# Moving the conditioning's multiplications from VectorE to ScalarE

## The chip, the cores and the metric

The kernel runs on one core of a Trainium2 chip. The metric is the device time of one execution in microseconds (us), lower is better. Work is issued in program order to five engines that run side by side: TensorE (PE; matmuls and, as PEld, weight loads), VectorE (DVE), ScalarE (ACT), GpSimd (POOL) and SyncE (SP). Each engine works through its own queue in order and waits on semaphores for the others. Transfers from HBM are issued from SP, ACT or POOL; a transfer stands in that engine's queue until its buffer is free, and then runs by itself.

## What the kernel computes

A two-layer encoder trunk on 256 tokens of width 1024. Each layer has a token mixer (three gated branches) and a PEER channel mixer (128x128 experts, top 16 of each of 8 heads). Both are conditioned by a vector c through adaLN:

```
cond = silu(c)
ada = cond @ w_ada[l] + b_ada[l]            # 1024 -> 6 x 1024, a matrix-vector product
sh1, sc1, g1, sh2, sc2, g2 = split(ada, 6)
u = x * (1 + sc1) + sh1;  x = LN(ALPHA * x + g1 * mixer(u))
u = x * (1 + sc2) + sh2;  x = LN(ALPHA * x + g2 * peer(u))
```

`w_ada` has 2 x 1024 x 6144 numbers, 50 MB. The change touches the product `cond @ w_ada` alone, and of it the part that is done beside other work.

## The kernel before

All large products are matmuls on TensorE in a split fp32 form. A weight tile of 128x1024 arrives by an SP transfer (`raw`, three buffers). ScalarE copies it to the rounded `hi` (L86), and VectorE or GpSimd subtracts to get `lo` (L88), as an item of the plan says ("v" or "g"). `Stream.get` (L98 to L110) does this two items ahead of TensorE: `hi` and `lo` have three buffers each, so the split of item i+2 starts when TensorE has finished item i-1, and the next `raw` load into a buffer waits until that item's split is done.

The stages in order: the mixer of layer 0 (projections, attention, long convolution, branches, output), up to about 400 us; PEER of layer 0, with the `u` stream (128 items against expert_u, to about 880 us) and the `v` stream (128 items against expert_v, L1550, to about 1240 us); then both again for layer 1. In the `v` loop each pair of items first prepares the two expert weights of the next pair: `hi` of P on ScalarE (L1494), `lo` of P on VectorE (L1495). Then each item is split ahead, multiplied (12 matmuls), and followed by one step of the conditioning, `self.ada(last, 1)` at L1523. In the same loop of layer 0, from about 1100 us on, the filters and loads of layer 1 run as background generators, pumped a step at a time (`self.bg.pump`).

The conditioning is cut into blocks (layer l, part j, half h) of eight tiles of 128x512, k = 0 to 7. The first two parts of layer 0 are done in `start` by other code. The other 20 blocks, 160 tiles, are done a tile at a time by `ada`, called once after each weight item in the mixer of layer 0 (L1095, L1120, L1140, L1165, L1216: 6 blocks), in the `v` loop of layer 0 (12 blocks) and at the beginning of that of layer 1 (2 blocks). The tiles have three buffers (`adaw`). A call at tile p first calls `ada_load` (L385), which issues, from the ACT queue, the transfers of all tiles up to p+2 that haven't been issued: in steady state one, that of tile p+2, into the buffer of tile p-1, for which it waits until VectorE has used tile p-1. Then VectorE multiplies tile p by column k of cond and adds it to the block's sum `acc` (one buffer): a TENSOR_SCALAR for k = 0 (L416), a SCALAR_TENSOR_TENSOR for the others (L418). After k = 7 one call does nothing and the next calls `ada_column` (L423): four PE transposes of `acc`, and two small VectorE operations. So a block takes ten calls.

Of the kernel before, what the change touches and what calls it, by code (L numbers as in the profile page):

```python
# [9 lines left out]
F32 = mybir.dt.float32  # L10
# [4 lines left out]
AF = mybir.ActivationFunctionType  # L15
ALU = mybir.AluOpType
# [140 lines left out]
class Trunk:  # L157
# [72 lines left out]
    def setup(self):  # L230
        nc, a = self.nc, self.a
        c = self.const
        self.ada_todo = [(l, j, k, h) for l in range(DEPTH) for j in range(6) for h in range(2) for k in range(8)
                         if (l, j) > (0, 1)]
        self.ada_tiles = {}
        self.ada_pos = self.ada_next = 0
        self.ada_done = None
        cc = c.tile([128, 8], F32, name="cc")
        self.load(cc, a["c"])
        self.ident = c.tile([128, 128], F32, name="ident")  # L240
        self.load(self.ident, a["ident"])
        self.bcol = c.tile([128, DEPTH, 6, 8], F32, name="bcol")
        self.load(self.bcol, a["bada"])
        self.new_x()
        self.open_layer(0)
        self.cond = c.tile([128, 8], F32, name="cond")
        e = c.tile([128, 8], F32, name="ce")
        nc.scalar.activation(out=e, in_=cc, func=AF.Exp, scale=-1.0)
        nc.vector.tensor_scalar(out=e, in0=e, scalar1=1.0, scalar2=None, op0=ALU.add)
        nc.vector.reciprocal(out=e, in_=e)  # L250
        nc.vector.tensor_tensor(out=self.cond, in0=cc, in1=e, op=ALU.mult)
        dp = self.ctx.enter_context(self.tc.tile_pool(name="dp", bufs=1, space=bass.MemoryType.DRAM))
        self.spill = dp.tile([128, 2, 1024], F32, name="spill")
        self.uh = self.keep.tile([128, 8, 256], F32R, name="uh")
        self.ul = self.keep.tile([128, 8, 256], F32R, name="ul")
        self.adac = c.tile([128, DEPTH, 6, 8], F32, name="adac")
        self.gbc = None
        for j in (1, 4):
            nc.vector.tensor_scalar(out=self.bcol[:, :, j, :], in0=self.bcol[:, :, j, :], scalar1=1.0, scalar2=None,
                                    op0=ALU.add)  # L260
# [134 lines left out]
    def ada(self, until, most=1000):  # L395

        nc = self.nc
        while most:
            if self.ada_done:
                self.ada_wait -= 1  # L400
                if self.ada_wait == 0 or most > 100:
                    self.ada_column()
                most -= 1
                continue
            if self.ada_pos == len(self.ada_todo) or self.ada_todo[self.ada_pos][:2] > until:
                return
            l, j, k, h = self.ada_todo[self.ada_pos]
            self.ada_load()
            w = self.ada_tiles.pop(self.ada_pos)
            self.ada_pos += 1  # L410
            most -= 1
            if k == 0:
                self.acc = self.sm.tile([128, 512], F32, tag="acc", name="acc", bufs=1)
            acc = self.acc
            if k == 0:
                nc.vector.tensor_scalar(out=acc, in0=w, scalar1=self.cond[:, 0:1], scalar2=None, op0=ALU.mult)  # L416
            else:
                nc.vector.scalar_tensor_tensor(out=acc, in0=w, scalar=self.cond[:, k:k + 1], in1=acc,  # L418
                                               op0=ALU.mult, op1=ALU.add)
            if k == 7:  # L420
                self.ada_done, self.ada_wait = (l, j, h), 2

    def ada_column(self):  # L423

        nc = self.nc
        l, j, h = self.ada_done
        self.ada_done = None
        s = slice(h * 4, h * 4 + 4)
        t = self.adac[:, l, j, s]
        p = self.bp((128, 4, 128))  # L430
        for m in range(4):
            nc.tensor.transpose(p[:, m, :], self.acc[:, m * 128:m * 128 + 128], self.ident)
        nc.vector.tensor_reduce(out=t, in_=p, op=ALU.add, axis=AX.X)
        nc.vector.tensor_tensor(out=t, in0=t, in1=self.bcol[:, l, j, s], op=ALU.add)
# [1269 lines left out]
```

## Time and profile before

| | |
|---|---|
| time, median of 3 runs | 2453.06 us (2447.99 to 2457.54) |
| the profiled execution's own time | 2454.66 us |
| its span, first to last instruction | 2452.6 us |
| mean granted clock of TensorE | 0.974 |
| PE busy | 2290.2 us, 93% |
| DVE busy | 1857.4 us, 76% |
| ACT busy | 1169.3 us, 48% |
| POOL busy | 874.7 us, 36% |
| DMA, mean | 179 GB/s |

Busy time is the time in which an engine executes an instruction, whether or not anything waits for it. The chain of waits says what the end hangs on: followed back from the last instruction, at each step to what released it. Its share of "issue" is time for which the profile shows no reason. The averages mix stages with different limits, so the views by stretch count more than this table.

### The profile page before, as it was taken

To read this page: it belongs to the slowest core of one execution; us is meant where nothing else is said; L and a number is where in the kernel's file an instruction comes from. 1 tells how busy PE (TensorE), PEld (TensorE's weight loads), DVE (VectorE), ACT (ScalarE), POOL (GpSimd) and SP (SyncE) were. 2 spreads that over 40 slices of the span, in tenths; PEclk is the share of its full clock that TensorE was granted. 3 is DMA by queue.
4 is the path that set the end of the run, shared out by engine and by line. 5 is a ranking of instruction groups with operands and counts; after the bars stand their busy time and mean duration, and the time that the engine had idled before them with its cause. 6 is when DMAs were issued, how large, how long until landed. Compare 5 with 4: busy or idle time off the path is not lost.

```text
span 2452.6 us, 38276 instructions
## 1 busy us (share of the span) xinstructions
PE 2290.2 (93%) x14400; PEld 2014.9 (82%) x14400; DVE 1857.4 (76%) x3196; ACT 1169.3 (48%) x1860; POOL 874.7 (36%) x403
## 2 busy tenths in 40 slices
PE   6899978979999999998899999899899999999997
PEld 4688657979999988885667886689899999888886
DVE  6886796977788878876975656879677887766676
ACT  4444434545555444443445444455455554444443
POOL 3521535660000024445754327557300000444563
PEclk9999998989999999998999999999999999999999
DMA  7553554545555578886664434444455555766664
GB/s 284 172 157 108 175 177 146 164 129 164 165 164 166 170 232 267 264 262 224 199 223 127 133 100 154 170 132 147 146 166 168 163 167 172 243 195 190 213 199 153
DMA packets 132592, 438.44 MB, mean 179 GB/s; under 512 B 16369, under 2 KB 17741, under 8 KB 130360
## 3 DMA queue, kind: packets, MB, share of 16 engines
q1 hardware_dynamic: 103328, 377.01, 48.6%
q10 hardware_dynamic: 26968, 51.23, 6.5%
q0 software_dynamic: 2112, 7.77, 0.9%
q8 instruction: 113, 1.85, 0.3%
q14 instruction: 71, 0.58, 0.1%
HBM read 432.80 MB, written 3.15 MB: 178 GB/s over the span
## 4 chain that ended last, share of the span: by engine, by line
PE 69%; DVE 21%; issue 3%; DMA 2%; ACT 2%; POOL 1%; ACTq 0%; SPq 0%; DVEq 0%; POOLq 0%
PE bg L209 26%; PE pj L1550 25%; PE pj L197 8%; DVE lo L88 2%; PE pj L209 2%; DVE acc L418 1%; DVE eq L1322 1%; PE gp L1449 1%; PE gp L1450 1%; PE bg L662 1%; ACT hi L86 1%; DVE eq L1317 1%; POOL lo L88 1%; DVE x L1254 1%; PE pj L1018 1%
## 5 line engine op out<-in xcount | busy, mean ns | idle before, releaser
L88 POOL TENSOR_TENSOR lo<-raw,hi 128x1024 fp32r<-128x1024 f32 x272 | 693.4, 2554 | 1489.0 <-ACT hi L86 1449.7
L86 ACT ACTIVATE hi<-raw 128x1024 fp32r<-128x1024 f32 x688 | 726.2, 1058 | 459.3 <-PE pj L1550 227.3
L209 PE MATMUL bg<-uh,hi 128*128 128x256 f32 x2240 | 645.0, 288 | 5.9 <-ACT hi L86 5.9
L1550 PE MATMUL pj<-hi,P 128*128 128x512 f32 x2048 | 641.6, 395 | 6.2 <-DVE P L1495 3.5
L88 DVE TENSOR_TENSOR lo<-raw,hi 128x1024 fp32r<-128x1024 f32 x416 | 543.9, 1308 | 134.2 <-ACT hi L86 127.9
L209 PE MATMUL bg<-uh,lo 128*128 128x256 f32 x2240 | 637.6, 285 | 8.2 <-POOL lo L88 8.2
L209 PE MATMUL bg<-ul,hi 128*128 128x256 f32 x2240 | 636.8, 284 | 0.0
L1550 PEld LDWEIGHTS pj<-hi,P 128*128 128x128 f32 x2048 | 387.2, 190 | 92.6 <-DVE P L1495 4.8
L209 PEld LDWEIGHTS bg<-uh,lo 128*128 128x128 f32 x2240 | 433.1, 193 | 9.4 <-POOL lo L88 9.4
L209 PEld LDWEIGHTS bg<-uh,hi 128*128 128x128 f32 x2240 | 433.4, 193 | 6.4 <-ACT hi L86 6.3
L209 PEld LDWEIGHTS bg<-ul,hi 128*128 128x128 f32 x2240 | 433.4, 193 | 0.1
L1550 PE MATMUL pj<-lo,P 128*128 128x512 f32 x1024 | 404.2, 395 | 12.2 <-DVE lo L88 8.0
L1495 DVE TENSOR_TENSOR P<-b,P 128x512 fp32r<-128x512 f32 x128 | 257.7, 2014 | 117.7 <-ACT P L1494 117.5
L1550 PEld LDWEIGHTS pj<-lo,P 128*128 128x128 f32 x1024 | 194.4, 190 | 58.9 <-DVE lo L88 11.6
L197 PE MATMUL pj<-hi,uh 128*128 128x512 f32 x432 | 190.6, 441 | 7.2 <-DVE mt L1175 3.1
L1479 ACT ACTIVATE bg<-bg 128x256 f32<-128x256 f32 (+24 forms) x208 | 56.8, 273 | 290.8 <-PE bg L209 290.8
L197 PE MATMUL pj<-lo,uh 128*128 128x512 f32 x432 | 176.0, 407 | 14.2 <-DVE lo L88 8.8
L197 PE MATMUL pj<-hi,ul 128*128 128x512 f32 x432 | 176.2, 408 | 9.0 <-DVE ul L1235 7.7
L418 DVE SCALAR_TENSOR_TENSOR acc<-adaw,cond,acc 128x512 f32<-128x512 f32 x140 | 141.1, 1008 | 4.1 <-DMA adaw<-in_wada 2.2
L1456 DVE SCALAR_TENSOR_TENSOR b<-gp,b 128x160 f32<-128x160 f32 (+6 forms) x236 | 58.8, 310 | 103.3 <-ACT b L1454 103.3
L197 PEld LDWEIGHTS pj<-lo,uh 128*128 128x128 f32 x432 | 85.4, 198 | 35.0 <-DVE lo L88 10.3
L197 PEld LDWEIGHTS pj<-hi,uh 128*128 128x128 f32 x432 | 85.1, 197 | 33.5 <-issue 7.4
(317 smaller groups left out, 2854.4 us busy)
## 6 DMA issues: line engine op xcount, KB each, us to landing
raw<-in_u SPq DMA_DIRECT2D x256, 512.0 KB, 3.5
raw<-in_v SPq DMA_DIRECT2D x256, 512.0 KB, 4.2
raw<-in_wtok SPq DMA_DIRECT2D x92, 512.0 KB, 3.6
adaw<-in_wada ACTq DMA_DIRECT2D x160, 256.0 KB, 3.7
raw<-in_whyd SPq DMA_DIRECT2D x24, 512.0 KB, 3.6
raw<-in_wq SPq DMA_DIRECT2D x24, 512.0 KB, 3.8
raw<-in_wbr SPq DMA_DIRECT2D x20, 512.0 KB, 3.7
su<-in_wada SPq DMA_DIRECT2D x8, 1024.0 KB, 10.5
```

What stands on the lines that cost most here:

```text
L86: self.nc.scalar.activation(out=h, in_=t, func=AF.Copy)
L88: eng.tensor_tensor(out=w, in0=t, in1=h.bitcast(F32), op=ALU.subtract)
L197: self.nc.tensor.matmul(psums[T], l[:, k, s], m[:, kk, :], start=(k == 0 and j == 0), stop=(k == K - 1 and j == 2))
L209: self.nc.tensor.matmul(ps, m[:, k, :], x[:, k, :], start=(k == 0 and j == 0), stop=(k == 7 and j == 2))
L418: nc.vector.scalar_tensor_tensor(out=acc, in0=w, scalar=self.cond[:, k:k + 1], in1=acc, op0=ALU.mult, op1=ALU.add)
L662: nc.tensor.matmul(ps[P], self.fwd[:, P, c, :], z[:, P, :], start=True, stop=True)
L1018: self.nc.tensor.matmul(ps[T], x[:, 2 * i + kk, ts], w[:, kk, :], start=x is self.uh and i + kk + part == 0, stop=x is self.ul and i + kk ...
L1254: nc.vector.max_index(out=i[:, 8:16], in_max=v[:, 8:16], in_values=s)
L1456: nc.vector.scalar_tensor_tensor(out=t[:, :, ts], in0=pr[:, i:j, :], scalar=1.0 / GATE_UNIT, in1=t[:, :, ts], op0=ALU.mult, op1=ALU.mult)
L1479: nc.scalar.activation(out=p[:, 0:n], in_=p[:, 0:n], func=AF.Gelu)
L1495: nc.vector.tensor_tensor(out=w, in0=src, in1=h.bitcast(F32), op=ALU.subtract)
L1550: self.nc.tensor.matmul(self.vacc[T][h], x[:, s], v[:, w], start=start and c == 0, stop=stop and c == 2)
```

## The change

`ada` no longer multiplies on VectorE. A new function `ada_product(i)` issues an ACTIVATE (Copy with the column of cond as a per-partition scale) on ScalarE: for k = 0 it writes the product straight into `acc`, for the others in place over the tile. A call at tile p makes sure that tile p has its product, and, unless p is the block's last, that of tile p+1 too. VectorE then adds tile p to `acc` with a TENSOR_TENSOR (nothing for k = 0). `ada_load` is now called from `ada_product`, only when a product is issued; what it loads is unchanged (all tiles up to two past the current one).

```diff
-        self.ada_pos = self.ada_next = 0
+        self.ada_pos = self.ada_next = self.ada_scaled = 0
 ...
             l, j, k, h = self.ada_todo[self.ada_pos]
-            self.ada_load()
+            self.ada_product(self.ada_pos)
+            if k < 7:
+                self.ada_product(self.ada_pos + 1)
             w = self.ada_tiles.pop(self.ada_pos)
             self.ada_pos += 1
             most -= 1
-            if k == 0:
-                self.acc = self.sm.tile([128, 512], F32, tag="acc", name="acc", bufs=1)
-            acc = self.acc
-            if k == 0:
-                nc.vector.tensor_scalar(out=acc, in0=w, scalar1=self.cond[:, 0:1], scalar2=None, op0=ALU.mult)
-            else:
-                nc.vector.scalar_tensor_tensor(out=acc, in0=w, scalar=self.cond[:, k:k + 1], in1=acc,
-                                               op0=ALU.mult, op1=ALU.add)
+            if k:
+                nc.vector.tensor_tensor(out=self.acc, in0=w, in1=self.acc, op=ALU.add)
             if k == 7:
                 self.ada_done, self.ada_wait = (l, j, h), 2
+
+    def ada_product(self, i):
+
+        if i < self.ada_scaled:
+            return
+        self.ada_scaled = i + 1
+        self.ada_load()
+        w, k = self.ada_tiles[i], self.ada_todo[i][2]
+        out = w
+        if k == 0:
+            out = self.acc = self.sm.tile([128, 512], F32, tag="acc", name="acc", bufs=1)
+        self.nc.scalar.activation(out=out, in_=w, func=AF.Copy, scale=self.cond[:, k:k + 1])
```

## Rows read from the trace of the kernel before

**Rows 1.** Busy time in three stretches: stretch, length, each engine, PEclk, DMA share, GB/s.
```profile
60.00:400.00 340.00, 297.95 (x1504) 237.80 (x1504) 266.86 (x436) 144.11 (x241) 135.67 (x60) 0.94 0.49 156
...
870.00:1100.00 230.00, 228.79 (x1056) 190.53 (x1055) 185.27 (x166) 110.78 (x129) 95.19 (x39) 1.00 0.81 261
1100.00:1260.00 160.00, 140.58 (x552) 103.89 (x551) 125.31 (x130) 71.79 (x90) 93.49 (x58) 0.94 0.68 219
```
**Rows 2.** The same stretches, VectorE's busy time on the conditioning's tiles alone.
```profile
60.00:400.00 340.00, 55.16 (x48) 0.94 0.49 156
...
870.00:1100.00 230.00, 45.66 (x64) 1.00 0.81 261
1100.00:1260.00 160.00, 40.58 (x32) 0.94 0.68 219
```
**Rows 3.** Chain of waits by line, 60 to 400 us, then 1100 to 1260 us.
```profile
by line: PE pj L197 27.8%; issue 10.7%; DVE acc L418 6.8%; DVE lo L88 5.9%; PE pj L209 5.2%; PE bg L662 4.0%; DMA raw<-in_wout 2.6%; DVE r L686 1.9%; DVE sq L629 1.8%; PE bg L604 1.8%; PE bg L753 1.5%; PE bg L809 1.5%; ACT hi L86 1.4%; PE b
...
by line: PE pj L1550 43.7%; issue 10.4%; DVE acc L418 7.1%; DMA w<-in_hy_w 5.5%; DVE lo L88 5.0%; PE bg L662 4.3%; DVE P L1495 3.2%; DMA adaw<-in_wada 3.2%; PE bg L604 3.0%; DVE sq L629 2.4%; DVE hh L578 2.1%; DVE acc L416 1.6%; POOL lo L88
```
**Rows 4.** Single lines on VectorE: ns min/median/max of one, first and last start.
```profile
L418 DVE SCALAR_TENSOR_TENSOR acc<-adaw,cond,acc x140: 735/751/2984, 76.1 to 2133.1; 128x512 f32<-128x512 f32 x140
L416 DVE TENSOR_SCALAR acc<-adaw,cond x20: 475/480/2614, 74.1 to 2116.3; 128x512 f32<-128x512 f32 x20
...
L1495 DVE TENSOR_TENSOR P<-b,P x128: 675/2467/4090, 879.5 to 2425.6; 128x512 fp32r<-128x512 f32 x128
```
**Rows 5.** Groups of instructions on ScalarE: count, busy us, mean ns, idle before.
```profile
L607 ACT ACTIVATE hh<-ld,nt 128x512 f32<-128x512 f32 x16 | 11.0, 720 | 6.7 <-DVE acc L418 6.7
...
L619 ACT ACTIVATE sq<-hh 128x512 f32<-128x512 f32 x16 | 9.5, 620 | 10.6 <-DVE acc L418 10.2 <-DVE sq L629 0.4
```
**Rows 6.** Transfers of adaw, issue to landing: 60 to 400, 870 to 1100, 1100 to 1260 us.
```profile
DMA to landing us min/median/max: 2.5/3.3/7.3
...
DMA to landing us min/median/max: 2.6/4.0/5.6
...
DMA to landing us min/median/max: 2.5/3.7/9.2
```
**Rows 7.** Timeline in the v stream: start, length, instruction, idle before; two items of a pair.
```profile
979.53 1.06 ACT L86 ACTIVATE hi<-raw 128x1024 fp32r<-128x1024 f32 x1 [1.14 <-PE pj L1550]
979.61 0.33 ACTq L392 DMA_DIRECT2D adaw<-in_wada  x1
...
980.83 1.21 DVE L88 TENSOR_TENSOR lo<-raw,hi 128x1024 fp32r<-128x1024 f32 x1
...
982.25 1.06 ACT L86 ACTIVATE hi<-raw 128x1024 fp32r<-128x1024 f32 x1 [1.66 <-PE pj L1550]
...
983.22 0.62 ACT L1494 ACTIVATE P<-b 128x512 fp32r<-128x512 f32 x1
...
983.39 2.41 POOL L88 TENSOR_TENSOR lo<-raw,hi 128x1024 fp32r<-128x1024 f32 x1 [3.03 <-ACT hi L86]
...
983.87 2.48 DVE L1495 TENSOR_TENSOR P<-b,P 128x512 fp32r<-128x512 f32 x1 [0.38 <-ACT P L1494]
```
**Rows 8.** Timeline where a block of the conditioning ends and the next begins.
```profile
955.08 0.34 ACTq L392 DMA_DIRECT2D adaw<-in_wada  x1
...
962.75 1.06 ACT L86 ACTIVATE hi<-raw 128x1024 fp32r<-128x1024 f32 x1 [1.14 <-PE pj L1550]
962.83 0.33 ACTq L392 DMA_DIRECT2D adaw<-in_wada  x1
...
965.88 1.06 ACT L86 ACTIVATE hi<-raw 128x1024 fp32r<-128x1024 f32 x1 [2.07 <-PE pj L1550]
...
967.02 2.42 POOL L88 TENSOR_TENSOR lo<-raw,hi 128x1024 fp32r<-128x1024 f32 x1 [3.45 <-ACT hi L86]
```
**Rows 9.** Who waited for whom, 870 to 1100, then 1100 to 1260: us, times, longest.
```profile
ACT hi L86 <- DMA raw<-in_v: 24.1, 14, 2.3
...
ACT P L1494 <- DVE acc L416: 7.3, 1, 7.3
```

## The prediction

> **What bounds the kernel now.** I read the busy time by stretch first, then the chain of waits of the stretches in which the conditioning runs, then its single instructions, then the timeline of the v stream. The 160 tiles fall into four places: 48 in the mixer of layer 0 (60 to 400 us), 64 in the saturated v stream (870 to 1100), 32 in its second half (1100 to 1260), 16 at the start of layer 1's v stream. The reader should see that these differ. From 870 to 1100 TensorE is busy 228.79 of 230 us at a granted clock of 1.00 [rows 1]: nothing taken from VectorE can shorten it. From 60 to 400 and 1100 to 1260 TensorE has gaps (297.95 of 340 us, 140.58 of 160) at a mean clock of 0.94, and VectorE is the fullest of the other engines (266.86 and 125.31 us) [rows 1]. There the conditioning is on the chain: L418 holds 6.8% of 340 us, 23.1 us, and L418 with L416 8.7% of 160 us, 13.9 us [rows 3], of the 55.2 and 40.6 us that VectorE spends on these tiles [rows 2]. Some 40% of such VectorE time counts; in the rest of the kernel none.
>
> **What the change takes off VectorE.** 140 times a SCALAR_TENSOR_TENSOR becomes a TENSOR_TENSOR of 128x512 f32 with both inputs in SBUF. The fastest of the one takes 735 ns, the fastest of the other kind 675 [rows 4]: 60 ns each. The slow ones (2984 against a median of 751) I read as waits for GpSimd's subtraction. That wait stays: L1495, the same TENSOR_TENSOR, has a median of 2467 ns, and in the timeline it runs from 983.87 to 986.35 beside a GpSimd operation that ends at 985.80 [rows 4, 7]. The page "SBUF — State Buffer" of the Trainium skill (section "Who interferes with whom") says the same: a VectorE instruction with two SBUF inputs competes for a port with a GpSimd instruction that reads SBUF, and whichever is later is fully blocked. By that rule the product leaves VectorE but the contended form stays; the 2467 ns agree.
>
> The 20 TENSOR_SCALARs (480 ns) go [rows 4]. In the two unsaturated stretches (70 adds, 10 blocks) that makes 70 x 0.060 + 10 x 0.480 = 9.0 us, of which 40% counts: **-3.6 us**. Bounds: 0 and -9.0.
>
> **What it adds to ScalarE.** 160 ACTIVATEs of 128x512 with a per-partition scale. The nearest row with such an operand, L607, takes 720 ns, without one (L619) 620 [rows 5]. I take 0.72: 115 us in all. In the saturated stretch 64 of them are 46 us, beside 110.78 us busy of 230 [rows 1]: hidden as work. In the other two stretches 80 are 58 us on an engine busy for 144.11 of 340 and 71.79 of 160 us. ScalarE's part of the chain there is small (`hi` has 1.4%) [rows 3]; at an estimated 4% for all its lines this is **+2.4 us**. Bounds: 0 and, if a third counted, 19.
>
> **The new wait inside a block.** In the call at tile p the ACT queue issues the transfer of p+2, and then has to run the product of p+1, whose transfer was issued one call earlier. Before, only VectorE waited for a tile, two calls after its issue. Calls in the v stream are 2.72 us apart (979.53 to 982.25), and a transfer takes a median of 4.0 us [rows 6, 7]. So ScalarE now stands. One pair worked through: the transfer issued at 979.61 lands at 983.6, its product runs to 984.3, and P (L1494), queued behind it, slides from 983.22 to 984.3. But L1495, which waits for P, can't finish before GpSimd's 985.80 whenever it starts; it still ends near 986.35. The next `hi` is due at 984.97 [rows 7] and gets its engine. So this wait is covered: **0**. It has no cover if landing takes about 5.6 us, the maximum [rows 6]; then `hi` comes 1.6 us late, against a margin that I work out next.
>
> **The new wait at the start of a block.** At k = 7 no product of p+1 is issued, and so no load. The transfer issued at k = 7 before (955.08) moves to the call at k = 0 (962.83) [rows 8], where two are now issued together: tile 1's and tile 2's. In that same call ScalarE must multiply tile 0 (long landed) and tile 1, whose transfer was issued just ahead. Everything behind stands for a whole landing: the next `hi`, `lo` behind that, P, the next transfers. At the median the product of tile 1 runs from 966.8 to 967.5, while the next `hi` was due at 965.88 [rows 6, 8]: 1.6 us late. What TensorE has left: `hi` starts when item i-1 is finished, and its `lo` is needed two items later, 5.44 us. On GpSimd the pair takes from 982.25 to 985.80, 3.55 us [rows 7]; the margin is 1.9. On VectorE (979.53 to 982.04) it is 2.9, but the item after tile 1's product is a GpSimd one [rows 7, 8]. So at the median landing nearly all margin goes, and at 5.6 us the delay is 3.2 and TensorE stands for 1.3. Two transfers at once should land later than single ones, and 14 of the `hi`s already wait for their own `raw` (24.1 us) [rows 9], whose reload is shifted as well. I take 0.8 us for each of the eight blocks of this stretch: **+6.4 us**. Bounds: 0 and 8 x 1.3 = 10.4.
>
> For the other 12 blocks (six, four and two) ScalarE's standing is about the median landing of 3.3 to 3.7 us and a product of 0.72 [rows 5, 6], around 4 us; where VectorE is the one that is late, much of it is idle time anyway (ScalarE is busy 42 to 45% there [rows 1]). Some waits also go: at k = 1 and at the old k = 7 place, the ACT queue no longer stands for VectorE's sum, as it did for 7.3 us once [rows 9]. Net I take 0.4 us each, the bottom of the 0 to 4 range: **+4.8 us**. Bounds: -14.6 (that 7.3 us and as much again) and +48.
>
> Sum: -3.6 + 2.4 + 0 + 6.4 + 4.8 = +10.0 us. On the profiled execution's 2454.66 (span 2452.6) that is 2464.7. This execution lay 1.6 us above the median of the runs, so I forecast **2463 us**, 10 above the median.
>
> The page "DMA: Bandwidth & Descriptors" of the Trainium skill (section "Rules for kernel authors") asks to issue a transfer early and wait for it late, which speaks against this change; its section "Anatomy of one DMA — SWDGE (gpsimd) path" prices one issued by GpSimd at about 2.0 us plus its bytes at 436 GB/s, an estimate of 2.6 us for 256 KB. By that price `hi` would be 0.2 us late at a block's start, inside the margin, and the sum would be 2457. The trace has 2.6 only as its minimum, and 4.0 as the median [rows 6], so the rows decide.
>
> **Rivals.**
> *Hidden.* The starts of blocks stay within the margin of 1.9 us, and the saving and ScalarE's work cancel: 2453 - 3.6 + 2.4 leaves 2452. For it: 1.6 is below 1.9, and ScalarE is half idle. Against: nothing is left for a second delay soon after.
>
> *Faster: the add escapes GpSimd.* If the add didn't meet GpSimd's operations, the time over its minimum would go too. The two stretches hold 95.7 us of VectorE time for these tiles [rows 2]; 70 adds at 0.675 are 47.3, so 48.5 us would go, 40% of it on the chain, 19 us; with +2.4 and +4.8 that is 2441. If a third of it comes true, 2453 - 6 = 2447. Against: L1495's median [rows 4].
>
> *Slower: ScalarE's standing is paid in full where TensorE isn't saturated.* Mechanism: ScalarE waits for the transfer just issued, and behind it, in order, stand the evacuations and `hi`s for which TensorE waits. It decides once two transfers at a time land after 4.5 us, or once ScalarE has no lead over TensorE at a block's start. Price: 8 x 1.3 and 12 x 2 (half of the 4), 10.4 + 24 - 3.6 + 2.4 = +33 us, 2486. For it: landings up to 7.3 and 9.2 us there [rows 6]. Against: VectorE, not ScalarE, is late there [rows 1, 3].
>
> **How the numbers follow.** My forecast has 0.50, hidden 0.15, slower 0.20, faster 0.15. A measurement of this kernel tells about 0.5%, 12 us, from no change: 2441 to 2465. The forecast's spread, 2455 to 2473, puts 0.28 within and 0.22 above; hidden adds 0.15 within, slower 0.20 above, faster 0.11 below and 0.04 within. So faster 0.11, same 0.47, slower 0.42. The range runs from 2446 (a part of the faster case) to 2485 (nearly all of the slower one).
>
> **What would show it.** L418 as a TENSOR_TENSOR with a minimum near 675 ns and still a maximum near 2.9 us; ACT up by about 115 us; new idle time of ScalarE "until DMA adaw", mainly 20 waits of 3 to 4 us in the calls at k = 0; TensorE gaps of around a microsecond in the saturated stretch, 27 us apart, with `lo` on GpSimd as their releaser; about 9 us less VectorE time in the other stretches. It is wrong if the stretch from 870 to 1100 keeps its length, if TensorE's gaps lie elsewhere, or if the adds' slow cases vanish.

## Result: 2488 us, slower by 1.5%

The changed kernel takes 2488.07 us (median of 4 runs, 2480.38 to 2491.55) against 2452.79 before (4 runs, 2447.99 to 2457.54): a ratio of 1.0149, 95% interval 1.0129 to 1.0168. I forecast 2463 and a range up to 2485; the sign was right, the size was not.

Four landmarks of the two profiles cut the span into five parts and say where its 37.1 us (2452.6 to 2489.7) went. The first matmul of the v stream of layer 0 comes at 882.5 instead of 879.5 us: +3.0 for everything up to there, the mixer with its 48 tiles included. From it to the first matmul of layer 1 (`pj<-e,uh`): 441.3 instead of 413.8, **+27.5**. From there to layer 1's v stream 792.3 instead of 791.9, +0.4. That stream, from its first matmul to the start of its last one on `hi`, 361.0 instead of 355.0, **+6.0**. The rest +0.2. The lines, each with the first and last start; first the kernel before, then the changed one:

```profile
L1550 PE MATMUL pj<-hi,P x59: 389/389/502, 879.5 to 899.9; 128*128 128x512 f32 x59
L1018 PE MATMUL pj<-e,uh x32: 389/389/774, 1293.3 to 1308.4; 128*128 128x512 f32 x32
L1550 PE MATMUL pj<-hi,P x1024: 387/389/502, 2085.2 to 2440.2; 128*128 128x512 f32 x171
```
```profile
L1558 PE MATMUL pj<-hi,P x50: 389/389/502, 882.5 to 899.7; 128*128 128x512 f32 x50
L1026 PE MATMUL pj<-e,uh x32: 389/393/776, 1323.8 to 1339.1; 128*128 128x512 f32 x32
L1558 PE MATMUL pj<-hi,P x1024: 387/389/632, 2116.1 to 2477.1; 128*128 128x512 f32 x171
```

So nearly all is lost in the two v streams, where I had put 6.4 of my 10 us plus shares of the others.

The stretches that answer to [rows 1], of the changed kernel (stretch, length, PE, PEld, DVE, ACT, POOL, granted clock, DMA share, GB/s):

```profile
60.00:400.00 340.00, 296.57 (x1499) 235.93 (x1499) 266.09 (x431) 172.66 (x285) 137.06 (x59) 0.94 0.48 156
870.00:1100.00 230.00, 217.15 (x971) 174.75 (x970) 154.68 (x143) 132.59 (x174) 86.22 (x35) 0.98 0.73 233
1100.00:1260.00 160.00, 133.92 (x541) 100.77 (x540) 116.00 (x122) 87.91 (x116) 90.57 (x58) 0.94 0.68 220
```

Look at the counts. From 60 to 400 us TensorE did 1499 matmuls instead of 1504. From 870 to 1100, the stretch that was saturated, it did 971 instead of 1056: 85 fewer in 230 us. No other engine is full there: VectorE is busy for 154.68 us instead of 185.27. That is what waiting looks like, and the waits name it (who waited for whom, 885 to 1085 us: us in total, times, longest):

```profile
ACT adaw L429 <- DMA adaw<-in_wada: 46.1, 20, 5.1
DVE P L1503 <- ACT P L1502: 29.0, 20, 3.9
ACT hi L86 <- DMA raw<-in_v: 25.0, 16, 3.2
DVE acc L415 <- ACT adaw L429: 24.4, 12, 5.3
PEld pj L1558 <- POOL lo L88: 13.5, 14, 2.1
ACT adaw L429 <- DVE acc L415: 12.0, 4, 3.7
PE pj L1558 <- POOL lo L88: 8.3, 7, 1.7
```

ScalarE stands for the conditioning's transfers, 46.1 us of 200; P and the adds stand behind ScalarE; and TensorE, which before had no wait here, stands for GpSimd's `lo`. The timeline shows it begin at a block's start and go on (ScalarE's queue in the changed kernel; in brackets the idle time before):

```profile
970.56 1.06 ACT L86 ACTIVATE hi<-raw 128x1024 fp32r<-128x1024 f32 x1 [1.68 <-DMA raw<-in_v]
970.59 0.82 ACTq L392 DMA_DIRECT2D adaw<-in_wada  x2
971.53 0.71 ACT L429 ACTIVATE acc<-adaw,cond 128x512 f32<-128x512 f32 x1
976.95 0.72 ACT L429 ACTIVATE adaw<-adaw,cond 128x512 f32<-128x512 f32 x1 [4.71 <-DMA adaw<-in_wada]
...
977.58 1.04 ACT L86 ACTIVATE hi<-raw 128x1024 fp32r<-128x1024 f32 x1
...
981.22 1.04 ACT L86 ACTIVATE hi<-raw 128x1024 fp32r<-128x1024 f32 x1
985.60 0.33 ACTq L392 DMA_DIRECT2D adaw<-in_wada  x1
985.99 0.72 ACT L429 ACTIVATE adaw<-adaw,cond 128x512 f32<-128x512 f32 x1 [3.73 <-DVE acc L415]
...
990.64 0.73 ACT L429 ACTIVATE adaw<-adaw,cond 128x512 f32<-128x512 f32 x1 [2.46 <-DMA adaw<-in_wada]
```

Two transfers are issued at 970.59, and the product of tile 1 waits for the first until 976.95: a landing of 6.3 us, and the next `hi`, due 2.7 us after the one before, comes 7.0 after it. Half a block later the queue stands again, this time with a transfer in front (985.60): its buffer is free only when VectorE has added the tile in it. That add ran into a GpSimd operation:

```profile
982.67 2.85 DVE L415 TENSOR_TENSOR acc<-adaw,acc 128x512 f32<-128x512 f32 x1
```
```profile
982.33 2.64 POOL L88 TENSOR_TENSOR lo<-raw,hi 128x1024 fp32r<-128x1024 f32 x1 [1.27 <-ACT hi L86]
```

The chain of waits from 880 to 1100 us, nearly all TensorE in the kernel before (first line), is now spread out (second line):

```profile
by line: PE pj L1550 98.5%; PE bg L432 1.4%; DVE P L1495 0.3%; issue 0.0%
```
```profile
by line: PE pj L1558 30.8%; DMA adaw<-in_wada 20.6%; issue 14.0%; DMA raw<-in_v 10.4%; POOL lo L88 7.6%; DVE acc L415 4.7%; DVE lo L88 3.9%; ACT hi L86 3.3%; ACT P L1502 2.0%; ACT adaw L429 1.3%; ACTq L392 1.1%; PE bg L440 0.8%; DVE P L1503
```

Not all of the loss is standing. From 885 to 1085 us the changed kernel does 95 matmuls fewer, as the next section shows. At the 0.223 us that one takes there in the kernel before (200 us over 898) these are worth 21 us. For 11 of them TensorE is idle (188.87 us busy of 200). In three places its granted clock falls as well. One is here, after TensorE had stood for 0.48 and 1.71 us within 3 us; the third line has its busy time from 980 to 985 us, in the order of the lines above:

```profile
978.67 0.73 PE L1558 MATMUL pj<-hi,P 128*128 128x512 f32 x2 [0.48 <-ACT hi L86]
981.11 0.50 PE L1558 MATMUL pj<-lo,P 128*128 128x512 f32 x1 [1.71 <-POOL lo L88]
980.00:985.00 5.00, 3.89 (x10) 3.07 (x11) 5.00 (x3) 2.26 (x3) 3.70 (x2) 0.66 0.50 164
```

The 0.66 is a mean over the clock's two levels, 1.2 and 2.4 GHz; the kernel before does 24 matmuls at 1.00 in these 5 us. The 5 us pieces of the stretch that lie below 1.00 (0.66, 0.66, 0.71 and 0.95) add up to an estimate of 5 us lost to the clock. The other 5 of the 21 us I can't place.

Single instructions of the changed kernel, for [rows 4 to 6]: the add, the product, and the transfers' landing from 885 to 1085 us.

```profile
L415 DVE TENSOR_TENSOR acc<-adaw,acc x140: 674/692/2935, 77.1 to 2174.3; 128x512 f32<-128x512 f32 x140
L429 ACT ACTIVATE adaw<-adaw,cond x140: 703/722/728, 75.1 to 2169.3; 128x512 f32<-128x512 f32 x140
...
DMA to landing us min/median/max: 2.8/4.3/7.2
```

### The profile page after: what moved, and what is told of

Read it like the earlier page. It is cut to its first block, busy times and chain, and to the rows that moved or that the text cites. A ratio compares the mean times of both kernels' runs of the same rounds, so it can differ in the third digit from the quotient of the medians.

```text
span 2489.7 us, 38244 instructions
## 1 busy us (share of the span) xinstructions
PE 2305.0 (93%) x14400; PEld 2018.2 (81%) x14400; DVE 1831.0 (74%) x3176; ACT 1265.1 (51%) x2020; POOL 879.2 (35%) x403
## 4 chain that ended last, share of the span: by engine, by line
PE 62%; DVE 22%; DMA 6%; issue 4%; ACT 3%; POOL 3%; ACTq 0%; POOLq 0%; DVEq 0%
PE bg L209 25%; PE pj L1558 18%; PE pj L197 8%; DVE lo L88 3%; DMA adaw<-in_wada 2%; POOL lo L88 2%; DMA raw<-in_v 2%; DVE acc L415 2%; PE pj L209 2%; DVE eq L1330 1%; PE gp L1457 1%; ACT hi L86 1%; PE gp L1458 1%; PE bg L670 1%; DMA w<-in_hy_w 1%
## 5 line engine op out<-in xcount | busy, mean ns | idle before, releaser
L1503 DVE TENSOR_TENSOR P<-b,P 128x512 fp32r<-128x512 f32 x128 | 211.9, 1656 | 141.6 <-ACT P L1502 141.3
L415 DVE TENSOR_TENSOR acc<-adaw,acc 128x512 f32<-128x512 f32 x140 | 176.8, 1263 | 48.9 <-ACT adaw L429 45.8
L429 ACT ACTIVATE adaw<-adaw,cond 128x512 f32<-128x512 f32 x140 | 100.5, 718 | 172.0 <-DMA adaw<-in_wada 106.3
```

The costliest lines, as they stand in the source:

```text
L415: nc.vector.tensor_tensor(out=self.acc, in0=w, in1=self.acc, op=ALU.add)
L429: self.nc.scalar.activation(out=out, in_=w, func=AF.Copy, scale=self.cond[:, k:k + 1])
L1503: nc.vector.tensor_tensor(out=w, in0=src, in1=h.bitcast(F32), op=ALU.subtract)
```

## The experiments

Theory A: ScalarE works in order and now waits for transfers that were issued too shortly before, and everything behind it is late. B: the added work itself. C: the loads wait for VectorE's adds, which now wait for ScalarE. For each kernel I give the time, its ratio (95% interval) to the kernel before on the same chip, and from its profile the *v time* (first matmul of layer 0's v stream to the first of layer 1; before 413.8, changed 441.3) and layer 1's v stream (before 355.0, changed 361.0). Both come from one profile of each kernel. The stretch between the two v streams, which no edit touches, takes 790.1 to 794.2 us in the twelve profiles, so I read nothing into differences under about 4 us. Where nothing else is said, the lines in fences are TensorE's and the others' busy time from 885 to 1085 us. There the kernel before does 898 matmuls and the changed one 803, as these two lines show, the first of before:

```profile
885.00:1085.00 200.00, 200.00 (x898) 165.65 (x897) 162.94 (x145) 95.72 (x109) 88.08 (x37) 1.00 0.83 266
```
```profile
885.00:1085.00 200.00, 188.87 (x803) 150.10 (x802) 134.29 (x122) 114.70 (x148) 78.84 (x32) 0.97 0.74 236
```

**The work alone**

```diff
# in the kernel before
             self.ada_load()
+            junk = self.sm.tile([128, 4, 128], BF16, tag="junk", name="junk", bufs=1)
+            nc.scalar.activation(out=junk, in_=self.ident.unsqueeze(1).to_broadcast([128, 4, 128]), func=AF.Copy,
+                                 scale=self.cond[:, k:k + 1])
```

> The kernel before, with one ScalarE product per tile added that waits for no transfer and feeds nobody (from the identity to a bfloat16 tile, 128x512, with the same per-partition scale, in the place in the queue where the change has its product). VectorE does all that it did. Theory A: 2451 to 2458, the work is hidden. Theory B: 2475 to 2490, the work alone makes most of the loss.

2456.72 us, 1.0021 (1.0005 to 1.0036); v time 414.1, layer 1's stream 354.8. In the saturated stretch TensorE loses nothing, with ScalarE at 132 us of 200:

```profile
885.00:1085.00 200.00, 200.00 (x897) 165.68 (x897) 148.57 (x145) 132.15 (x167) 91.44 (x37) 1.00 0.84 266
```

B falls: 160 products that wait for no transfer cost 0.2% (at most 0.4% by the interval), and nothing in the v streams.

**The product in its own tile's call**

```diff
             self.ada_product(self.ada_pos)
-            if k < 7:
-                self.ada_product(self.ada_pos + 1)
```

> The changed kernel, but each product is issued in its own tile's call instead of one call ahead: two calls now lie between a transfer's issue and ScalarE's wait for it, as they did for VectorE before. ScalarE's added work and VectorE's adds stay. Theory A (ScalarE stands, in order, for transfers that were issued too shortly before): most of the 35 us come back, 2450 to 2462. Theory B (the added 0.72 us products themselves hold up the hi copies): stays at 2480 to 2490. Theory C (the loads wait for VectorE's adds, which now wait for ScalarE): stays slow too or gets slower, 2480 to 2500, since an add now follows its product at once.

2456.32 us, 1.0021 (1.0008 to 1.0033); v time 417.6, layer 1's stream 354.5. All work is as in the changed kernel. The distance between issue and wait has gone from one call to two. Since each call now has its own product, each also issues one load, so no two are issued together at k = 0. TensorE is full again:

```profile
885.00:1085.00 200.00, 200.00 (x898) 165.72 (x897) 142.52 (x138) 133.03 (x168) 88.44 (x37) 1.00 0.82 265
```

That VectorE's add now follows its product at once does little harm (3.8 us of v time), so the wait for the product alone isn't it. Nor are slow adds the cause: 72 of them take over 1 us here, each beside a GpSimd operation (42 in the changed kernel), and all take 197.3 us (176.8 there, 141.1 before), with hardly any loss:

```profile
L413 DVE TENSOR_TENSOR acc<-adaw,acc 128x512 f32<-128x512 f32 x140 | 197.3, 1409 | 97.5 <-ACT adaw L427 97.5
```

**Loads in every call**

```diff
             l, j, k, h = self.ada_todo[self.ada_pos]
+            self.ada_load()
             self.ada_product(self.ada_pos)
```

> The changed kernel, but the loads are issued at every call, at k = 7 too, so that no two transfers are issued together at k = 0 and tile 1 of a block is in flight for three calls before its product. Inside a block nothing changes. Theory A1 (the starts of blocks are the cause, the rest is their aftermath): 2455 to 2465. Theory A2 (the one-call distance inside a block is enough by itself): 2475 to 2488, a third or less comes back. Theory B: no change, 2486 to 2490.

2461.38 us, 1.0039 (1.0025 to 1.0054); v time 423.4, layer 1's stream 354.5. So 17.9 of the 27.5 us and all of layer 1's 6.0 go when tile 1 is on its way before k = 0; 9.6 stay with the one-call distance inside blocks.

```profile
885.00:1085.00 200.00, 197.21 (x879) 161.61 (x878) 138.42 (x134) 126.52 (x162) 85.74 (x35) 1.00 0.82 258
```

**No product of tile 1 in the call of tile 0**

```diff
-            if k < 7:
+            if 0 < k < 7:
                 self.ada_product(self.ada_pos + 1)
```

> The changed kernel without the product of tile 1 in the call of tile 0; that call still issues two loads together, and the call of tile 1 makes the products of tiles 1 and 2. If it is the wait for the transfer just issued at a block's start that sets the delay going: 2458 to 2468, about as with loads in every call (2461). If it is the two transfers at once, which take longer to land: 2475 to 2488.

2465.35 us, 1.0052 (1.0036 to 1.0069); v time 426.2, layer 1's stream 355.1. The two transfers are still issued together, yet 15.1 of the 27.5 us go: it is mainly the wait for what was just asked for, not the pair.

```profile
885.00:1085.00 200.00, 198.43 (x880) 161.57 (x879) 138.71 (x133) 125.70 (x160) 87.58 (x35) 1.00 0.81 258
```

**Without the adds**

```diff
-            if k:
+            if k == 7:
                 nc.vector.tensor_tensor(out=self.acc, in0=w, in1=self.acc, op=ALU.add)
```

> The changed kernel without VectorE's adds for k = 1 to 6 (the conditioning's sums are left out; only the add at k = 7 stays). Loads into a buffer now wait for ScalarE's product alone. Theory A: ScalarE's waits stay, so the loss in the saturated stretch stays: 2470 to 2488 (a little is gained from 120 adds of 0.69 us on VectorE). Theory C: the loss goes, 2440 to 2455.

2457.0 us, 1.0029 (1.0013 to 1.0044). This total misleads, and neither theory had it right. The first matmul of the v stream comes at 866.8 instead of 882.5: in the mixer, where VectorE is on the chain, leaving the adds out gains 15.7 us. The v time is 423.9, still 10.1 above before, and ScalarE still waits for transfers:

```profile
ACT adaw L429 <- DMA adaw<-in_wada: 42.0, 21, 4.4
```

Layer 1's stream takes 355.5. So A holds without any add, but for about 10 us, and the adds have a part in the other 17.

**Adds that don't hold the buffers**

```diff
             if k:
-                nc.vector.tensor_tensor(out=self.acc, in0=w, in1=self.acc, op=ALU.add)
+                nc.vector.tensor_tensor(out=self.acc, in0=self.acc, in1=self.acc, op=ALU.max)
```

> The changed kernel with each add replaced by a VectorE operation of the same form and size that reads the sum twice and not the tile (the sums over k are left out). VectorE is as full as before; loads into a buffer wait for ScalarE's product alone. If the adds' release of buffers made the difference between the changed kernel and the one without adds: like that one in the v stream of layer 0 (424 us from its first matmul to the next layer's first). If VectorE's fullness made it: like the changed kernel there (441 us), about 2485 in all.

2472.56 us, 1.0102 (1.0070 to 1.0134); v time 428.3, layer 1's stream 354.9. VectorE is as full as in the changed kernel (142.46 us of 200, against 134.29), but 13.0 of the 27.5 us are gone:

```profile
885.00:1085.00 200.00, 192.50 (x849) 156.66 (x850) 142.46 (x131) 124.63 (x161) 84.91 (x34) 1.00 0.78 251
```

So most of the adds' part isn't that VectorE is full. This edit takes away two waits at once, that of the loads for the adds and that of VectorE for the products (24.4 us of 200 in the changed kernel); the next pair separates them. It may be a mixture all the same (428.3 against 423.9 without adds, hardly more than the spread). The total lies higher since the v stream begins at 885.5 here.

**A fourth buffer, with and without more distance**

```diff
+        n = 4 if self.ada_four else 3          # second kernel: 3 if self.ada_four else 3
-        while self.ada_next < min(self.ada_pos + 3, len(self.ada_todo)):
+        while self.ada_next < min(self.ada_pos + n, len(self.ada_todo)):
...
+            if self.ada_four and i % 4 == 3:
+                t = self.sel.rearrange("p a t r -> p (a t r)")[:, 0:1024].bitcast(F32)
+            else:
-            t = self.sm.tile([128, 512], F32, tag="adaw", name="adaw", bufs=3)
+                t = self.sm.tile([128, 512], F32, tag="adaw", name="adaw", bufs=3)
...
             for p in range(len(vseq)):
+                self.ada_four = 2 <= p < len(vseq) - 6
```

> The same fourth buffer, but loads still issued two calls ahead, two together at k = 0: only a load's wait for the add of the tile three places before it goes away. If this release by the late adds keeps a delay alive that the start of a block set going: about the time with the adds elsewhere, 424 to 430 us for the v stream of layer 0, and layer 1's without loss; 2464 to 2474 in all. If release is no part of it: 438 to 442 us, 2483 to 2490.

2474.53 us, 1.0086 (1.0064 to 1.0108); v time 424.5, layer 1's stream 356.0. Of the changed kernel's 27.5 us 16.8 go when a load no longer waits for the add of the tile three places before, with the near waits unchanged and VectorE still waiting for the products. Release does keep the delay alive; in that part theory C is right.

```profile
885.00:1085.00 200.00, 195.50 (x865) 159.15 (x865) 147.90 (x132) 125.88 (x162) 86.11 (x35) 1.00 0.79 255
```

> The changed kernel with a fourth buffer for the conditioning's tiles in the v streams (in a tile that is idle there), and loads issued three calls ahead instead of two: two calls between a transfer's issue and ScalarE's product, and tile 1 of a block on its way before k = 0. The mixer's part is as changed. If near transfers, waited for in ScalarE's queue, are the cause: the v stream of layer 0 takes 414 to 419 us from its first matmul to the next layer's (changed 441, before 414), and the whole 2453 to 2461. If ScalarE's work or VectorE's fullness is: 435 and more, 2480 and more.

2463.43 us, 1.0041 (1.0024 to 1.0057); v time 416.5, layer 1's stream 356.7. With a call more of distance 24.8 of 27.5 go, and the saturated stretch is full:

```profile
885.00:1085.00 200.00, 199.78 (x896) 165.50 (x896) 143.84 (x138) 132.53 (x168) 88.47 (x36) 1.00 0.83 268
```

The v time met the forecast in both. Both totals lie just above theirs, 2463.43 against 2461 and 2474.53 against 2474, with the v stream beginning at 884.5 and 884.6 in the profiles. The mixer's code is that of the changed kernel (882.5), so a few us between profiles there are not explained by any edit.

**The kernel before, with loads one call ahead**

```diff
# in the kernel before
-        while self.ada_next < min(self.ada_pos + 3, len(self.ada_todo)):
+        while self.ada_next < min(self.ada_pos + 2, len(self.ada_todo)):
```

> The kernel before with its loads one call ahead instead of two: VectorE now waits for a transfer that was issued one call earlier, and ScalarE for none. If one call of 2.72 us is too near for any engine that waits in order: 2470 to 2490. If it is ScalarE's waiting that hurts, since the hi copies are queued behind it: 2453 to 2462.

2456.78 us, 1.0030 (1.0017 to 1.0044); v time 413.8, layer 1's stream 354.3. VectorE now waits 33.2 us for these transfers (2.2 before), and TensorE stays full:

```profile
885.00:1085.00 200.00, 200.00 (x898) 165.68 (x897) 158.92 (x143) 95.26 (x109) 90.79 (x37) 1.00 0.82 265
```

The 0.3% lie outside the v streams, and no landmark places them. One call is near enough here, where VectorE waits (19.8 us from 885 to 1085) and no `hi` stands behind it. The comparison isn't exact: ScalarE waits longer in the changed kernel (46.1 us), and with loads one call ahead a load needs an add from two calls before, not from the call before, so the release of buffers isn't put to the test.

**The loads on SP's queue**

```diff
-            self.nc.scalar.dma_start(out=t, in_=self.a["wada"][l, j, k, h])
+            self.nc.sync.dma_start(out=t, in_=self.a["wada"][l, j, k, h])
```

> The changed kernel with the conditioning's transfers issued from the SP queue instead of ScalarE's. A load no longer stands behind a product that waits in ScalarE's queue; products, their places and the buffers stay, so at a block's start ScalarE still waits for a transfer just asked for. If the loss in the v stream comes from loads that stand behind waiting products, two tiles to a landing: 2458 to 2470. If ScalarE's wait at a block's start does it whatever the queue: 2475 to 2490. If SP's raw loads stand behind the adds for which these loads wait: 2490 and more.

2640.27 us, 1.0773 (1.0751 to 1.0795); v time 549.7, layer 1's stream 379.8. The time of the third case, and by far more, but for another reason: not `raw` loads that stand behind the adds, but the reverse. A transfer of the conditioning now stands in SP's queue behind `raw` loads, and those wait for `lo`, 160.2 us of 200 (who waited for whom in SP's queue, 885 to 1085 us):

```profile
SPq L67 <- POOL lo L88: 102.0, 17, 7.1
SPq L67 <- DVE lo L88: 58.2, 29, 3.5
SPq L392 <- DVE P L1503: 0.8, 4, 0.2
```

ScalarE's waits for it grow from 107.3 to 373.6 us over the kernel; so each `hi` is later, and each `lo`, and each `raw` load:

```profile
964.05 0.33 SPq L67 DMA_DIRECT2D raw<-in_v  x1
964.42 0.43 SPq L392 DMA_DIRECT2D adaw<-in_wada  x1
966.39 0.33 SPq L67 DMA_DIRECT2D raw<-in_v  x1
966.76 0.43 SPq L392 DMA_DIRECT2D adaw<-in_wada  x1
972.46 0.33 SPq L67 DMA_DIRECT2D raw<-in_v  x1
972.88 0.38 SPq L392 DMA_DIRECT2D adaw<-in_wada  x1
```

Each time in these lines the conditioning's load leaves 0.4 us after a `raw` load, never alone, with up to 6 us from one pair to the next.

## Why the prediction was wrong

*The sign and the kind of wait* were right: a product waits for its transfer in ScalarE's queue, at a block's start for one just asked for. *VectorE's saving* was right in size (minimum 674 against 735 ns, median 692 against 751) and, as forecast, the contended form stayed (maximum 2935). But over the kernel the adds' time went up, from 141.1 to 176.8 us in 140 instructions: moved in time, they met GpSimd's operations more often. ScalarE's waits for transfers aren't needed for that: with the product in its own tile's call, where these waits are 1.5 us over the kernel, the adds take 197.3 us. All 42 adds of the changed kernel over 1 us lie beside a GpSimd operation, as do all 22 of the kernel before, though some short ones do too. The port rule of the page "SBUF — State Buffer" of the Trainium skill (section "Who interferes with whom") says that a VectorE instruction with two SBUF inputs contends with a GpSimd instruction that reads SBUF. The trace agrees.

*ScalarE's work* was right: 0.72 us each, and nearly hidden (the work-alone kernel, 0.2%).

*The new wait inside a block: 0.* This step failed. I followed one pair from a state without delay, found the wait covered, and priced it at nothing. I did not follow what a late pair does to the next. With the starts of the blocks out of the way (loads in every call) the wait inside the blocks still costs 9.6 us of v time, and it carries on what a start begins. Three buffers serve a tile's whole way: transfer (median 4.3 us), product (0.72), add (0.69, or 2.9 beside GpSimd), and then the next transfer into the same buffer; three calls are 8.16 us. On time, that fits: 5.7 us, or 7.9 with a slow add. With a landing of 6.3 us, as at the start of a block, and a slow add it is 9.9. And in the ACT queue transfer p+2 stands before product p+1, and `hi` behind both, so once late, the late `hi` makes the late add, that the late load, and that the late product. In the timeline of the changed kernel the queue stands again at 985.99 and 990.64, 15 and 20 us after the start of the block. So ScalarE waits for these transfers 55 times over the kernel, 107.3 us in all, where I had expected mainly 20 waits; TensorE's gaps do end with `lo` on GpSimd, as forecast (8.3 of 11.0 us). Taking away either the cause (loads in every call: -17.9) or the carry (a fourth buffer: -16.8) removes about two thirds; more distance with the fourth buffer removes 24.8. In each of the three the granted clock is 1.00 in the saturated stretch, so some 5 of the us that each brings back are the clock's, and the parts can't be added up.

*The start of a block: 0.8 us each.* It was mis-sized. The 17.9 us that loads in every call bring back are 1.5 us for each of the 12 blocks, above my bound of 1.3; two transfers together took 6.3 us to land where my longest was 5.6, and the aftermath counts with it. The 95 missing matmuls, 21 of the 27.5 us, lie in 200 us of the saturated stretch, where I had put 6.4 in all.

*The other twelve blocks: 4.8 us.* The two in layer 1's stream cost 6.0 us, where I had put 0.8. The six of the mixer cost 3.0 us by the landmark at 882.5, and about 5 by the two fourth-buffer kernels, whose mixer has the same code (884.5 and 884.6): not told apart from the 2.4 that I gave them. The four late blocks of the v stream of layer 0 I can't separate.

*The rivals.* The slower one (0.20) had the right total, 2486, for a half right reason: the mechanism was the wait it named, but it laid 24 of its 33 us on stretches where TensorE isn't saturated, so its total is right by luck. The profile's most comfortable stretch, TensorE at 228.79 of 230 us [rows 1], is the one that lost most: where TensorE is always busy, nothing makes up the time for which it stands. VectorE has little room there too, 185.27 us busy of 230 [rows 1]; how much that adds isn't shown.

What stays open: the last 2.7 to 3.8 us of the v time in the two kernels that come nearest (within the spread named above), the mixer's part, and 5 of the 21 us in the saturated stretch.

## What to carry to other kernels

When work moves to another engine, ask first what stands behind it in that engine's queue. Waits for near transfers cost nothing in the v streams on VectorE (33.2 us over the kernel, 0.3% in all); on ScalarE, where they are 107.3 us and each `hi` stands behind them, they are the main part of 1.5%. The page "DMA: Bandwidth & Descriptors" of the Trainium skill (section "Rules for kernel authors") says to issue a transfer early and wait for it late. The runs agree: with the product one call after its transfer's issue the change cost 35 us, and moving it one call later returned 31. Cost a wait in a ring of buffers not from the state without delay but from the late one: add up one buffer's whole round, and see whether it leaves room to catch up.

## What the runs showed beyond that

Issuing a transfer from another engine's queue "to get it out of the way" can tie two streams together: on SP's queue the same 160 transfers take 187 to 190 us more than the kernel before, some 152 of them beyond what the change itself costs, while the DMA engines are less busy (share 0.54 from 885 to 1085 us, against 0.83). And in the mixer VectorE's time on the conditioning counts about as I had priced it. The 42 adds there hold 54.4 us of VectorE in the changed kernel; without 36 of them 7.6 are left, and the v stream begins 15.7 us earlier (866.8 against 882.5). That is 34% of the 46.8 us taken away, where I had counted 40%, though some waits of ScalarE go with them:

```profile
60.00:400.00 340.00, 54.41 (x42) 0.94 0.48 156
```
```profile
60.00:400.00 340.00, 7.62 (x6) 0.95 0.49 159
```
